# Attention in two halves of the queries: maximum, softmax, values and copies of the result

## The chip, the cores and the metric

The kernel runs on one core of a Trainium2 chip. A core has a matrix engine (TensorE, PE in the profile; its weight loads are listed as PEld), three engines for elementwise work (VectorE or DVE, ScalarE or ACT, GpSimd or POOL) and a queue engine (SyncE or SP) that here only starts transfers; 16 DMA engines move the data. Each engine works through its own instructions in order, and semaphores between them say when an operand is ready or a buffer free. Matrix products are summed in eight PSUM banks of 128 partitions x 512 columns; everything else sits in SBUF or, for larger things, in DRAM. The metric is the time of one execution on the device in microseconds (us), the median of three runs.

## The reference

A decoder trunk of two layers on x (1024 positions x 1024 channels). Layer 0 mixes with a gated short convolution, layer 1 with dilated attention; each is followed by a SwiGLU feed-forward net, with RMS norms in between. The change touches only the attention of layer 1:

```python
qkv = (h @ w_qkv).reshape(bsz, seq, 3, N_HEADS, HEAD_DIM)      # 16 heads of 64
for window, dilation in ((128, 1), (512, 4), (2048, 16)):
    o, l = dilated_branch(q, k, v, rel_bias, window, dilation)  # banded, causal, with a bias by distance
    outs.append(o); lses.append(l)                              # o normalised, l = log of the sum of exponentials
alpha = softmax(lses)                                           # over the three branches
o = sum(alpha * outs)
x = x + o @ w_out
```
Since the branches are weighted by their own sums of exponentials, the result for a query is one softmax over the keys of all three branches together: the sum of exp(score - maximum) * v over the sum of exp(score - maximum).

## The kernel before

Everything outside the attention is the same before and after. A matrix product in fp32 is done as three products of rounded parts: `split` (L135) makes of a tile its high part (a copy on ScalarE, L145) and the low part that is left (a subtract on VectorE, L146), and TensorE adds hi*hi, hi*lo and lo*hi (L373, L374, L375). Weights reach the products through `take` (L174) and `ensure` (L166): a slab is loaded (`load_raw`, SP, L159), split, and taken one slab ahead of its use. SBUF tiles are "pages" from a pool of 41, PSUM tiles "banks" from a ring of 8: whoever wants a bank waits until the one eight before it has been read. The order of the code is the order on each engine.

The attention (L1480) runs heads in 17 slots, n = 0 to 16 (`slot`, L1717). In slot n stand the scores of head n, the softmax and value products of head n-1, and "dense" filler for TensorE, taken in steps from a generator (`other`, `fill`): the value projections, the last projections of q and k, and at the end the first half of the output product (`out_product`), which adds to x with L492.

For one head, with keys on the 128 partitions and the 1024 queries in the columns:

- `scores` (L1561): products of key classes and queries (L1574, L1575) fill banks, and VectorE moves them out with the bias added into four tiles: lf (1024 columns) and lh (512) for the two coarser branches, ld and lp for the finest. While that goes on VectorE takes the maximum of the tiles per column into m (L1599, L1620 to L1625). Then POOL reduces m over the partitions into mb (`partition_all_reduce`, L1628), all 1024 columns at once.
- `softmax` (L1631): five pairs of a subtract of mb on VectorE (L1636) and an exponential on ScalarE (L1637), for lf, lh, ld and two pieces of lp. One pair is issued per step of the next slot up to slot 13 (`LAG`), all five together after that.
- `values` (L1640): products of the exponentials with vx (L1647) into two banks acc[0] and acc[1], one for each half of the queries. Both banks are taken at the start. The order is lf for both halves, lh, then ld and lp. vx holds, for each of 16 key blocks, the values of head a=0, 64 columns of ones, and the values of head a=1, so that a window of 128 columns gives the weighted values of one head in 64 rows and the sum in the other 64. At the end ScalarE takes for both halves the logarithm of the sums into z (L1670) and copies the values into o (L1671), and so frees the banks.
- `finish` (L1674) and `attended` (L1707): z becomes 1/sum by an exponential, o is multiplied with it (L1711), and the pair of heads goes to DRAM (odram, POOL's queue, L1712).

vx is one buffer, filled by `load_values` (L1530) for each pair of heads, on SP: six transfers in pieces of 256 bytes (64 values), the first three into the columns of head a=0, the last three into those of head a=1. The columns of a=0 are free once the first head of the old pair has done its products, those of a=1 only when the second has. On the same queue stand the loads of q and k (`load_kq`, L1539), of the bias (`load_bias`, L1465), of weights, and of finished pairs for the output product (`load_attended`, L1796, the tiles oin). The first four pairs are read at the start of slot 11 and split, one per step, by `halves` (L1839).

Of the kernel before, what the change touches and what calls it, by code (L numbers as in the profile page):

```python
# [52 lines left out]
FILL = (("v", 0), ("v", 1), ("v", 2), ("v", 3), ("qk", 7))  # L53
DENSE = (13,) * 13 + (16, 13, 12, 11)
# [47 lines left out]
def trunk(ctx: ExitStack, tc: tile.TileContext, x, gains_in, cwi, ck, cwo, wqkv, wo, relb,  # L102
# [32 lines left out]
    def split(src, dst=None, eng=nc.vector):  # L135

        w = src.shape[1]
        if dst is None:
            if w <= HALF:
                t = page("w", F32R)  # L140
                dst = t[:, :w], t[:, HALF:HALF + w]
            else:
                dst = page("w_hi", F32R)[:, :w], page("w_lo", F32R)[:, :w]
        hi, lo = dst
        nc.scalar.activation(hi, src, AF.Copy)  # L145
        eng.tensor_tensor(out=lo, in0=src, in1=hi, op=ALU.subtract)  # L146
        return hi, lo

# [25 lines left out]
    def take(key, ahead=1):  # L174
        i = op_state[1]
        assert ops[i][0] == key, (ops[i][0], key)
        ensure(i + ahead)
        op_state[1] += 1
        return made.pop(i)
# [1300 lines left out]
    def attention(norm, qk):  # L1480
# [5 lines left out]
        vx = scope["pool"].tile([128, 16, 192], F32, name="vx", tag="vx", bufs=1)  # L1486
        nc.vector.memset(vx[:, :, 64:128], 1.0)
# [41 lines left out]
        def load_values(p):  # L1529
            src = vdram[p // 2]  # L1530
            for a in range(2):
                off = src.offset + p % 2 * 128 + a * 64
                dims = slice(128 * a, 128 * a + 64)
                nc.sync.dma_start(vx[:, 0:8, dims], bass.AP(src.tensor, off, [[256, 128], [128 * 256, 8], [1, 64]]))
# [26 lines left out]
        def scores(p, a, st):  # L1561
# [40 lines left out]
            for j in range(0, 8, 2):  # L1602
# [22 lines left out]
            nc.vector.tensor_tensor(out=m[:, HALF:], in0=m[:, HALF:], in1=lp[:, HALF:], op=ALU.max)  # L1625
            mb = page("mb")
            st["mb"] = mb
            nc.gpsimd.partition_all_reduce(mb, m, 128, bass_isa.ReduceOp.max)  # L1628
            yield

        def softmax(st):  # L1631
            lf, lh, ld, lp, mb = (st[n] for n in ("lf", "lh", "ld", "lp", "mb"))
            for dst, m in ((lf, mb), (lh, mb[:, HALF:]), (ld, mb),
                           (view(lp, 8, [[32, 16], [1, 24]]), view(mb, 8, [[32, 16], [1, 24]])),
                           (lp[:, HALF:], mb[:, HALF:])):
                nc.vector.tensor_tensor(out=dst, in0=dst, in1=m, op=ALU.subtract)  # L1636
                nc.scalar.activation(dst, dst, AF.Exp)  # L1637
                yield

        def values(p, a, st):  # L1640
            lf, lh, ld, lp = (st[n] for n in ("lf", "lh", "ld", "lp"))
            acc = [bank(), bank()]
# [3 lines left out]
            def mm(ih, off, dims, u, rhs, first=False, last=False):  # L1646
                nc.tensor.matmul(view(acc[ih], off, dims), vx[:, u, 64 * a:64 * a + 128], rhs,  # L1647
                                 start=first, stop=last)

            for ih in range(2):  # L1650
                for r4 in range(4):
# [3 lines left out]
            for r4 in range(4):  # L1655
                mm(1, r4 * 32, kd, 12 + r4, view(lh, r4 * 32, kd))
                if r4 % 2:
                    yield
            for j in range(8):
                off = (j % 4) * 8  # L1660
                mm(j // 4, off, b1, j, view(ld, blk(j), b1), last=False)
                if j:
                    mm(j // 4, off, b1, j - 1, view(lp, blk(j), b1), last=j % 4 == 3)
                yield
            o, z = st["o"], st["z"]
            n0 = slice(64 * a, 64 * a + 64)
            z0 = slice(64 - 64 * a, 128 - 64 * a)
            for ih in range(2):
                s = slice(ih * HALF, (ih + 1) * HALF)
                nc.scalar.activation(z[n0, s], acc[ih][z0], AF.Ln)  # L1670
                nc.scalar.activation(o[n0, s], acc[ih][n0], AF.Copy)  # L1671
            yield
# [44 lines left out]
        def slot(n, dense, ndense, late=0, hook=iter(())):  # L1717

            def other(k):
                for _ in range(k):  # L1720
                    next(dense, None)
# [80 lines left out]
        def split_attended(raw):  # L1802
            return {p: split(t) for p, t in raw.items()}
# [35 lines left out]
        def halves():  # L1839
            for q, t in done.items():  # L1840
                first[q] = split(t)
# [12 lines left out]
        run(dense)  # L1854
        return acts
# [180 lines left out]
```

## Time and profile before

| | us |
|---|---|
| median of three runs | 2103.54 (2102.79, 2103.54, 2103.99) |
| the profiled execution | 2105.08 |
| its span, first to last instruction | 2103.3 |
| TensorE busy | 2083.1 (99%), granted clock 0.998 |
| VectorE, ScalarE, POOL busy | 1746.1 (83%), 1013.7 (48%), 240.0 (11%) |
| the attention's slots | about 1105 to 1475 of the span |

The profile comes from one execution, 1.54 us above the median. A row of a timeline gives start, duration, engine, line of the kernel, operation, output <- inputs with their sizes, how many instructions are drawn together (x8), and in brackets how long the engine stood idle before and on whom it waited. A line of the waits names the waiting instruction, whom it waited for, and the total, the number and the longest of these waits. A row of a group (by line and tile) gives shortest, median and longest duration in ns.

### The profile page before, as it was taken

The numbers are of one execution on the slowest core, as the hardware profiler recorded it, in microseconds if no ns is written. First come the engines' busy times: TensorE is split into PE (matmuls) and PEld (weight loads), VectorE is DVE, ScalarE is ACT, GpSimd is POOL, SyncE is SP. The second block draws the span as 40 slices with busy tenths as digits, with TensorE's granted clock in tenths as the row PEclk, the third lists the DMA queues.
The fourth block names the chain that finished last, engine by engine and source line by source line (L and its number), as shares of the span: only waits on it lengthen the run. The fifth ranks groups of instructions, "written<-read, shape, count | busy, mean of one in ns | idle before, by whom it ended". The sixth has DMA issues, their size and how long they took to land. (4 is left out here: it accounts for less than half of the span.)

```text
span 2103.3 us, 30766 instructions
## 1 busy us (share of the span) xinstructions
PE 2083.1 (99%) x10990; PEld 1792.2 (85%) x10990; DVE 1746.1 (83%) x3264; ACT 1013.7 (48%) x1852; POOL 240.0 (11%) x336
## 2 busy tenths in 40 slices
PE   9999999999999999999999999999999999999998
PEld 7788888888888888887789999988788888888887
DVE  8898769988888788968984778987998888888886
ACT  7433427444444454445553566555544434456433
POOL 1000000110101010010223232211011001001000
PEclk9999999999999999999999999999999999999999
DMA  7322643233333467452658788955223323368432
GB/s 216 100 96 71 230 135 76 101 105 111 102 105 110 145 201 208 133 159 65 232 201 209 161 202 210 250 165 154 71 87 108 107 99 113 110 194 245 158 96 80
DMA packets 141495, 300.70 MB, mean 143 GB/s; under 512 B 48236, under 2 KB 54462, under 8 KB 141344
## 3 DMA queue, kind: packets, MB, share of 16 engines
q1 hardware_dynamic: 107488, 201.94, 32.4%
q0 software_dynamic: 26224, 82.11, 12.6%
q10 hardware_dynamic: 7632, 14.70, 1.9%
q8 instruction: 87, 1.43, 0.3%
q14 instruction: 64, 0.52, 0.1%
HBM read 208.42 MB, written 82.93 MB: 139 GB/s over the span
## 5 line engine op out<-in xcount | busy, mean ns | idle before, releaser
L573 PE MATMUL bank<-b,w 128*128 128x512 f32 x1980 | 772.5, 390 | 5.4 <-DVE w L146 5.2
L571 PE MATMUL bank<-b,w 128*128 128x512 f32 x1980 | 772.3, 390 | 2.3 <-ACT w L145 1.1
L572 PE MATMUL bank<-b,w 128*128 128x512 f32 x1980 | 771.9, 390 | 0.6 <-DVE b L882 0.6
L573 PEld LDWEIGHTS bank<-b,w 128*128 128x128 f32 x1980 | 372.0, 188 | 87.5 <-DVE w L146 10.5
L571 PEld LDWEIGHTS bank<-b,w 128*128 128x128 f32 x1980 | 372.3, 188 | 80.3 <-ACT w L145 1.9
L572 PEld LDWEIGHTS bank<-b,w 128*128 128x128 f32 x1980 | 372.3, 188 | 76.6 <-DVE b L882 1.2
L145 ACT ACTIVATE w<-combo 128x512 fp32r<-128x512 f32 (+2 forms) x492 | 251.5, 541 | 238.9 <-DVE combo L193 219.7
L146 DVE TENSOR_TENSOR w<-combo,w 128x512 fp32r<-128x512 f32 (+2 forms) x492 | 279.8, 582 | 37.8 <-ACT w L145 37.0
L577 ACT ACTIVATE part<-bank 128x512 f32<-128x512 f32 x189 | 112.5, 595 | 383.9 <-PE bank L573 378.7
L146 DVE TENSOR_TENSOR w<-raw,w 128x512 fp32r<-128x512 f32 (+2 forms) x345 | 194.4, 585 | 36.5 <-ACT w L145 36.5
L581 DVE TENSOR_TENSOR part<-part,bank 128x256 f32<-128x256 f32 (+1 forms) x369 | 173.1, 499 | 31.9 <-PE bank L573 17.3
L145 ACT ACTIVATE w<-raw 128x512 fp32r<-128x512 f32 (+2 forms) x345 | 168.5, 531 | 47.8 <-PE bank L573 12.2
L373 PE MATMUL bank<-w_hi,w 128*128 128x512 f32 (+1 forms) x400 | 151.0, 378 | 0.1
L375 PE MATMUL bank<-w_hi,w 128*128 128x512 f32 (+1 forms) x400 | 149.3, 373 | 0.7 <-DVE w L146 0.7
L374 PE MATMUL bank<-w_lo,w 128*128 128x512 f32 (+1 forms) x400 | 149.0, 373 | 0.0
L801 DVE TENSOR_TENSOR x<-x,bank 128x512 f32<-128x512 f32 x136 | 92.9, 683 | 28.7 <-PE bank L573 28.7
L492 DVE TENSOR_TENSOR x<-x,bank 128x512 f32<-128x512 f32 (+1 forms) x104 | 66.7, 644 | 59.8 <-PE bank L375 58.9
L193 DVE TENSOR_TENSOR combo<-raw 128x512 f32<-128x512 f32 (+1 forms) x174 | 112.6, 648 | 0.0
L375 PEld LDWEIGHTS bank<-w_hi,w 128*128 128x128 f32 x400 | 75.3, 188 | 14.8 <-DVE w L146 1.6
L564 DVE TENSOR_TENSOR b<-hin,b 128x512 fp32r<-128x512 f32 x126 | 79.5, 686 | 9.4 <-ACT b L563 9.4
L373 PEld LDWEIGHTS bank<-w_hi,w 128*128 128x128 f32 x400 | 75.5, 189 | 12.3 <-ACT w L145 0.5
L374 PEld LDWEIGHTS bank<-w_lo,w 128*128 128x128 f32 x400 | 75.5, 189 | 11.9
(234 smaller groups left out, 3377.0 us busy)
## 6 DMA issues: line engine op xcount, KB each, us to landing
hin<-part SPq DMA_DIRECT2D x126, 256.0 KB
raw<-in_ffn_w_gate SPq DMA_DIRECT2D x44, 512.0 KB
raw<-in_ffn_w_up SPq DMA_DIRECT2D x44, 512.0 KB
part<-sum POOLq DMA_DIRECT2D x72, 256.0 KB, 2.3
raw<-in_ffn_w_down SPq DMA_DIRECT2D x48, 384.0 KB
raw<-in_attn_w_qkv SPq DMA_DIRECT2D x27, 512.0 KB
raw<-in_conv_w_in SPq DMA_DIRECT2D x24, 512.0 KB
part<-part POOLq DMA_DIRECT2D x36, 256.0 KB, 2.6
```

The costliest lines, as they stand in the source:

```text
L145: nc.scalar.activation(hi, src, AF.Copy)
L146: eng.tensor_tensor(out=lo, in0=src, in1=hi, op=ALU.subtract)
L193: eng.tensor_tensor(out=c, in0=a, in1=b, op=op)
L373: nc.tensor.matmul(b, whi[:, a], ahi[:, s], start=first, stop=False)
L374: nc.tensor.matmul(b, whi[:, a], alo[:, s], start=False, stop=False)
L375: nc.tensor.matmul(b, wlo[:, a], ahi[:, s], start=False, stop=last)
L571: nc.tensor.matmul(b, hi[:, a], bhi, start=start and k == 0, stop=False, skip_group_check=True)
L572: nc.tensor.matmul(b, hi[:, a], blo, start=False, stop=False, skip_group_check=True)
L573: nc.tensor.matmul(b, lo[:, a], bhi, start=False, stop=k == n - 1, skip_group_check=True)
L577: nc.scalar.activation(t, b, AF.Copy)
L581: nc.vector.tensor_tensor(out=t, in0=t, in1=b, op=ALU.add)
L801: nc.vector.tensor_tensor(out=X[n][:, half(h)], in0=X[n][:, half(h)], in1=b, op=ALU.add)
```

## The change

Four things change, all within the attention.

*Halves of the queries.* The maximum is reduced in two pieces of 512 columns: the first as soon as ld and lp of queries 0 to 511 are in m, in the middle of the scores, the second after the last scores. The softmax becomes seven pairs instead of five, in the order lf, ld, lp of half 0, then lf, lh, ld, lp of half 1. The value products go by halves too: acc[0] is taken, gets lf, ld and lp, and its z and o follow at once; only then acc[1] is taken.

*Values in 512-byte pieces.* vx is laid out as ones, head 0, head 1, ones, head 0, and so on, with 17 blocks of ones, so that the 128 values of a pair lie side by side. `load_values` is three transfers instead of six, in pieces of 512 bytes. Sums and values change rows, and z and o with them.

*Low parts later.* While the attention runs, the subtract of a `split` is put on a list and issued at the next filler step or the next `take`.

*Reads of finished pairs.* oin of pairs 0 and 1 is read and split in slot 10, that of 2 and 3 in slot 11, in SP's order behind the loads of q, k and bias of that slot.

```diff
@@ split @@
         nc.scalar.activation(hi, src, AF.Copy)
-        eng.tensor_tensor(out=lo, in0=src, in1=hi, op=ALU.subtract)
+        low = lambda: eng.tensor_tensor(out=lo, in0=src, in1=hi, op=ALU.subtract)
+        if behind[0]:
+            lows.append(low)
+        else:
+            low()
...
+    behind, lows = [False], []
+
+    def flush_lows():
+        while lows:
+            lows.pop(0)()
@@ take @@
+        flush_lows()
         ensure(i + ahead)
+        if i + 1 > state0:
+            flush_lows()
@@ attention, load_values @@
-        vx = scope["pool"].tile([128, 16, 192], F32, name="vx", tag="vx", bufs=1)
-        nc.vector.memset(vx[:, :, 64:128], 1.0)
+        vx = scope["pool"].tile([128, 16 * 192 + 64], F32, name="vx", tag="vx", bufs=1)
+        nc.vector.memset(view(vx, 0, [[192, 17], [1, 64]]), 1.0)
...
-            for a in range(2):
-                off = src.offset + p % 2 * 128 + a * 64
-                dims = slice(128 * a, 128 * a + 64)
-                nc.sync.dma_start(vx[:, 0:8, dims], bass.AP(src.tensor, off, [[256, 128], [128 * 256, 8], [1, 64]]))
-                for h in range(2):
-                    nc.sync.dma_start(vx[:, 8 + 4 * h:12 + 4 * h, dims],
-                                        bass.AP(src.tensor, off + 512 * 256 * h, [[1024, 128], [256, 4], [1, 64]]))
+            off = src.offset + p % 2 * 128
+            nc.sync.dma_start(view(vx, 64, [[192, 8], [1, 128]]),
+                              bass.AP(src.tensor, off, [[256, 128], [128 * 256, 8], [1, 128]]))
+            for h in range(2):
+                nc.sync.dma_start(view(vx, (8 + 4 * h) * 192 + 64, [[192, 4], [1, 128]]),
+                                  bass.AP(src.tensor, off + 512 * 256 * h, [[1024, 128], [256, 4], [1, 128]]))
@@ scores @@
                     nc.vector.tensor_tensor(out=q(m), in0=q(m), in1=q(lp), op=ALU.max)
+                    mb = page("mb")
+                    st["mb"] = mb
+                    nc.gpsimd.partition_all_reduce(mb[:, :HALF], m[:, :HALF], 128, bass_isa.ReduceOp.max)
...
-            mb = page("mb")
-            st["mb"] = mb
-            nc.gpsimd.partition_all_reduce(mb, m, 128, bass_isa.ReduceOp.max)
+            nc.gpsimd.partition_all_reduce(mb[:, HALF:], m[:, HALF:], 128, bass_isa.ReduceOp.max)
@@ softmax @@
-            for dst, m in ((lf, mb), (lh, mb[:, HALF:]), (ld, mb),
+            for dst, m in ((lf[:, a], mb[:, a]), (ld[:, a], mb[:, a]),
                            (view(lp, 8, [[32, 16], [1, 24]]), view(mb, 8, [[32, 16], [1, 24]])),
-                           (lp[:, HALF:], mb[:, HALF:])):
+                           (lf[:, b], mb[:, b]), (lh, mb[:, b]), (ld[:, b], mb[:, b]), (lp[:, b], mb[:, b])):
@@ values @@
-            acc = [bank(), bank()]
+            acc = {}
...
             for ih in range(2):
+                acc[ih] = bank()
                 for r4 in range(4):
                     mm(ih, r4 * 32, kd, 8 + r4, view(lf, ih * HALF + r4 * 32, kd), first=r4 == 0)
...
+                for r4 in range(4 * ih):
+                    mm(1, r4 * 32, kd, 12 + r4, view(lh, r4 * 32, kd))
...
+                for j in range(4 * ih, 4 * ih + 4):
+                    off = (j % 4) * 8
+                    mm(ih, off, b1, j, view(ld, blk(j), b1), last=False)
+                    if j:
+                        mm(ih, off, b1, j - 1, view(lp, blk(j), b1), last=j % 4 == 3)
                     yield
...
+                nc.scalar.activation(z[n0, half(ih)], acc[ih][n0], AF.Ln)
+                nc.scalar.activation(o[n0, half(ih)], acc[ih][o0], AF.Copy)
                 yield
@@ slot @@
             def other(k):
                 for _ in range(k):
+                    flush_lows()
                     next(dense, None)
...
                 bias[n + 1] = load_bias(n + 1)
+            done.update(load_attended(ps))
@@ the loop over the slots @@
+        behind[0] = True
         for n in range(H):
-            if n == LAG - 2:
-                done.update(load_attended(range(AO)))
-            hook = halves() if n == LAG - 2 else iter(())
-            slot(n, dense, DENSE[n], 3 if n == H - 2 else 0, hook)
+            ps = {OIN - 1: (0, 1), OIN: (2, 3)}.get(n, ())
+            hook = halves(ps)
+            slot(n, dense, DENSE[n], 3 if n == H - 2 else 0, hook, ps)
```

How the order moves is shown at three places. The first is ScalarE from slot 13 into slot 14, with the exponentials of head 13 and z and o of head 12. Before (lf_12950 to lp_12953 are head 13's; banks 13058 and 13059 are head 12's two halves):

```order
L1637 ACTIVATE lf_12950<-lf_12950 128x1024
L1637 ACTIVATE lh_12951<-lh_12951 128x512
L1637 ACTIVATE ld_12952<-ld_12952 128x1024
L1637 ACTIVATE lp_12953<-lp_12953 128x16x24
L1637 ACTIVATE lp_12953<-lp_12953 128x512
L145 ACTIVATE w_13100<-raw_12869 128x512
L1670 ACTIVATE z_12947<-bank_13058 64x512
L1671 ACTIVATE o_12946<-bank_13058 64x512
L1670 ACTIVATE z_12947<-bank_13059 64x512
L1671 ACTIVATE o_12946<-bank_13059 64x512
```
After (lf_12990 to lp_12993 are head 13's; banks 13103 and 13129 are head 12's halves):

```order
L1684 ACTIVATE z_12987<-bank_13103 64x512
L1685 ACTIVATE o_12986<-bank_13103 64x512
L1652 ACTIVATE lf_12990<-lf_12990 128x512
L1652 ACTIVATE ld_12992<-ld_12992 128x512
L1652 ACTIVATE lp_12993<-lp_12993 128x16x24
L1652 ACTIVATE lf_12990<-lf_12990 128x512
L1652 ACTIVATE lh_12991<-lh_12991 128x512
L1652 ACTIVATE ld_12992<-ld_12992 128x512
L1652 ACTIVATE lp_12993<-lp_12993 128x512
L146 ACTIVATE w_13149<-raw_12912 128x512
L1684 ACTIVATE z_12987<-bank_13129 64x512
L1685 ACTIVATE o_12986<-bank_13129 64x512
```
z and o of the first half have moved ahead of all exponentials of head 13; those of the second half still stand behind them and behind a weight's copy.

The second place is VectorE over the end of the same head's scores (m is the maximum per column, mb the reduced one, bias rows are evictions of banks). Before:

```order
L1611 TENSOR_TENSOR ld_12952<-bank_13029,bias_12752 128x16x16
L1616 TENSOR_TENSOR lp_12953<-bank_13029,bias_12752 128x16x16
L1611 TENSOR_TENSOR ld_12952<-bank_13039,bias_12752 128x16x16
L1616 TENSOR_TENSOR lp_12953<-bank_13039,bias_12752 128x16x8
L1624 TENSOR_TENSOR m_12988<-m_12988,ld_12952 128x512
L1625 TENSOR_TENSOR m_12988<-m_12988,lp_12953 128x512
L492 TENSOR_TENSOR x_12778<-x_12778,bank_13010 128x512
L1636 TENSOR_TENSOR lf_12950<-lf_12950,mb_13051 128x1024
```
After (the first half's all-reduce waits for the first row shown; lines are 13 higher, softmax's 15):

```order
L1635 TENSOR_TENSOR m_13028<-m_13028,lp_12993 128x16x24
L147 TENSOR_TENSOR w_13045<-raw_12522,w_13045 128x512
L1651 TENSOR_TENSOR ld_12797<-ld_12797,mb_12879 128x512
L1624 TENSOR_TENSOR ld_12992<-bank_13073,bias_12790 128x16x16
L1629 TENSOR_TENSOR lp_12993<-bank_13073,bias_12790 128x16x16
L1651 TENSOR_TENSOR lp_12798<-lp_12798,mb_12879 128x512
L1624 TENSOR_TENSOR ld_12992<-bank_13085,bias_12790 128x16x16
L1629 TENSOR_TENSOR lp_12993<-bank_13085,bias_12790 128x16x8
L1640 TENSOR_TENSOR m_13028<-m_13028,ld_12992 128x512
L1641 TENSOR_TENSOR m_13028<-m_13028,lp_12993 128x512
L506 TENSOR_TENSOR x_12816<-x_12816,bank_13049 128x512
L1651 TENSOR_TENSOR lf_12990<-lf_12990,mb_13064 128x512
```
Head 12's last subtracts (ld_12797, lp_12798) and a weight's low part now stand between the start of the first reduce and the last four evictions of head 13's scores.

The third place is SP's queue in slot 11. Before:

```order
L1799 DMA oin<-odram_85 128x1024
L1799 DMA oin<-odram_86 128x1024
L1799 DMA oin<-odram_87 128x1024
L1799 DMA oin<-odram_88 128x1024
L1546 DMA ka<-kq_1_2926 64x1024
L1547 DMA ka<-kq_1_2926 64x1024
L1534 DMA vx<-vdram_95 128x8x64
L1536 DMA vx<-vdram_95 128x4x64 x2
L1534 DMA vx<-vdram_95 128x8x64
L1536 DMA vx<-vdram_95 128x4x64 x2
```
After (the first row is the last load of slot 10):

```order
L1815 DMA oin<-odram_86 128x1024
L170 DMA raw<-in_attn_w_out 128x512 x2
L1559 DMA ka<-kq_1_2926 64x1024
L1560 DMA ka<-kq_1_2926 64x1024
L1546 DMA vx<-vdram_95 128x8x128
L1549 DMA vx<-vdram_95 128x4x128 x2
L1564 DMA qa<-kq_0_2925 64x1024 x2
L1565 DMA ql_10192<-kq_0_2925 64x1024
L1482 DMA bias<-tables 128x1x361
L1483 DMA bias<-tables 128x1x349
L1815 DMA oin<-odram_87 128x1024
L1815 DMA oin<-odram_88 128x1024
```
Three rows of vx stand where six did (a row x2 counts for two), and two of the four loads of finished pairs come at the end of the slot instead of ahead of it.

More of the change, by code (lines that the diff above doesn't have):

```diff
@@ L53 @@
 FILL = (("v", 0), ("v", 1), ("v", 2), ("v", 3), ("qk", 7))
+OIN = LAG - 2
 DENSE = (13,) * 13 + (16, 13, 12, 11)
@@ L1715, in attention, with slot @@
         OZ, acts = {}, {}
-        def slot(n, dense, ndense, late=0, hook=iter(())):
+        def slot(n, dense, ndense, late=0, hook=iter(()), ps=()):
             def other(k):
                 for _ in range(k):
+                    flush_lows()
                     next(dense, None)
@@ L1802, in split_attended @@
         def split_attended(raw):
-            return {p: split(t) for p, t in raw.items()}
+            done = {p: split(t) for p, t in raw.items()}
+            flush_lows()
+            return done
         def out_product(g, ps, acts):
@@ L1837, in fill, with halves @@
             yield from out_product(0, range(AO), first)
-        def halves():
-            for q, t in done.items():
-                first[q] = split(t)
+        def halves(ps):
+            for q in ps:
+                first[q] = split(done.pop(q))
                 yield
         dense = fill()
+        behind[0] = True
         for n in range(H):
-            if n == LAG - 2:
-                done.update(load_attended(range(AO)))
-            hook = halves() if n == LAG - 2 else iter(())
-            slot(n, dense, DENSE[n], 3 if n == H - 2 else 0, hook)
+            ps = {OIN - 1: (0, 1), OIN: (2, 3)}.get(n, ())
+            hook = halves(ps)
+            slot(n, dense, DENSE[n], 3 if n == H - 2 else 0, hook, ps)
             run(hook)
@@ L1854, in attention @@
         run(dense)
+        flush_lows()
+        behind[0] = False
         return acts
```

26 lines of the change are left out of this document (8 added, 18 removed).

## The prediction

> **What bounds the kernel now.** I read the page's busy times first, then the waits of TensorE inside the attention, then busy time by stretch, then the timelines around the one place where TensorE stands still, and last VectorE's waits and the DMA shares, since the change touches these.
>
> ```profile
> span 2103.3 us, 30766 instructions
> PE 2083.1 (99%) x10990; PEld 1792.2 (85%) x10990; DVE 1746.1 (83%) x3264; ACT 1013.7 (48%) x1852; POOL 240.0 (11%) x336
> ```
> TensorE is busy for 99% of the span. The change neither adds nor drops a matmul, so it can only win idle time of TensorE, and only inside the attention (about 1105 to 1475 us). How much is there?
>
> ```profile
> PE bank L1574 <- ACT o L1671: 0.8, 1, 0.8
> ...
> 1145.00:1300.00 155.00, 155.00 (x1291) 152.70 (x1290) 118.74 (x222) 93.15 (x132) 47.95 (x39) 1.00 0.76 183
> 1300.00:1350.00 50.00, 50.00 (x344) 45.92 (x343) 47.41 (x76) 30.42 (x41) 14.55 (x10) 1.00 1.02 262
> ...
> 1365.00:1370.00 5.00, 4.24 (x35) 3.97 (x34) 4.09 (x7) 4.80 (x9) 0.00 (x0) 1.00 0.55 126
> ...
> 1403.00:1405.00 2.00, 1.96 (x14) 1.47 (x13) 2.00 (x4) 1.84 (x3) 0.00 (x0) 1.00 0.24 82
> ...
> sum 370.00, PE 369.21 PEld 346.26 DVE 285.09 ACT 208.19 POOL 90.40; mean PE 46.15 PEld 43.28 DVE 35.64 ACT 26.02 POOL 11.30
> ```
> The first line is the only wait that TensorE has there. The others are busy times by stretch (PE, weight loads, DVE, ACT, POOL, clock, DMA share, GB/s): 370.00 - 369.21 = 0.79 us idle in the whole attention, 0.76 of it between 1365 and 1370. The granted clock is 1.00 throughout, so nothing is to be won there. VectorE is full only in 1300:1350, 47.41 of 50.00 us, where the DMA is saturated too (share 1.02).
>
> The idle 0.76 us, on TensorE, ScalarE, VectorE and POOL in turn:
>
> ```profile
> 1367.28 1.05 PE L1647 MATMUL bank<-lf,vx 128*128 128x128 f32 x8
> 1369.09 0.33 PE L1574 MATMUL bank<-qa,kca 128*128 128x128 f32 x1 [0.76 <-ACT o L1671]
> ...
> 1363.70 1.06 ACT L1637 ACTIVATE lf<-lf 128x1024 f32<-128x1024 f32 x1 [5.39 <-DVE lf L1636]
> 1366.40 1.03 ACT L1637 ACTIVATE lp<-lp 128x384 f32<-128x384 f32 x2
> 1367.34 0.61 ACT L145 ACTIVATE w<-raw 128x512 fp32r<-128x512 f32 x1
> 1367.86 0.58 ACT L1670 ACTIVATE z<-bank 64x512 f32<-64x512 f32 x1
> 1368.44 0.59 ACT L1671 ACTIVATE o<-bank 64x512 f32<-64x512 f32 x1
> ...
> 1358.33 0.69 DVE L1625 TENSOR_TENSOR m<-m,lp 128x512 f32<-128x512 f32 x1
> 1362.44 1.23 DVE L1636 TENSOR_TENSOR lf<-lf,mb 128x1024 f32<-128x1024 f32 x1 [2.82 <-POOL mb L1628]
> ...
> 1359.18 3.22 POOL L1628 PARTITION_ALL_REDUCE mb<-m  x1 [13.12 <-DVE m L1625]
> ```
> The last row of head 13's maximum ends at 1359.02. POOL's all-reduce takes 3.22 us, VectorE waits 2.82 for it, ScalarE 5.39, and head 13's five exponentials stand ahead of head 12's z and o in ScalarE's order. So the bank of head 12's first query half comes free at 1368.44 + 0.59 = 1369.03, and the scores of head 14 start at 1369.09.
>
> **The change, part by part.** *Order on ScalarE.* Now z and o of head 12's first half stand ahead of head 13's exponentials, and that bank is wanted one bank later in the ring. Those of the second half stay behind seven exponentials and a weight copy, but this bank is only wanted by head 13's second half, taken after scores that now start at 1369.09. When are they done? The second half's all-reduce starts near 1359.2 and takes between 1.6 us (half of 3.22, if it goes by columns) and 3.22 (if it is all fixed cost), then four subtracts, one exponential, the weight copy and z and o:
>
> ```profile
> L1636 DVE TENSOR_TENSOR lf<-lf,mb x16: 1209/1226/1227, 1136.4 to 1401.6; 128x1024 f32<-128x1024 f32 x16
> L1636 DVE TENSOR_TENSOR lh<-lh,mb x16: 681/682/687, 1138.2 to 1402.7; 128x512 f32<-128x512 f32 x16
> ...
> L1637 ACT ACTIVATE lf<-lf x16: 1050/1061/1065, 1137.7 to 1402.8; 128x1024 f32<-128x1024 f32 x16
> L1637 ACT ACTIVATE lh<-lh x16: 612/632/635, 1139.0 to 1403.8; 128x512 f32<-128x512 f32 x16
> ```
> 4 x 0.68 + 0.63 + 0.61 + 0.58 + 0.59 = 5.1, so 1365.9 to 1367.5: 1.6 us or more before 1369.09. The stall goes: **-0.76 us**. The idle 0.04 us at 1403 (TensorE meets the last head's exponentials) should go too, since the last head's first half is ready sooner: -0.04, which I round to a sum of -0.8.
>
> *More instructions.* Per head lf and ld become two pieces each: VectorE pays 2 x (2 x 0.682 - 1.22) = +0.29 us, ScalarE 2 x (2 x 0.632 - 1.061) = +0.41, over 16 heads 4.6 and 6.5 us. Cover: of the 370 us VectorE works 285.09 and ScalarE 208.19. That cover is thin only in 1300:1350, with 2.59 us of VectorE left for three heads, of which 0.9 is now taken. What VectorE gains there against it:
>
> ```profile
> DVE lf L1636 <- POOL mb L1628: 32.9, 13, 3.5
> ...
> L1628 POOL PARTITION_ALL_REDUCE mb<-m x16 | 55.9, 3496 | 142.8 <-DVE m L1625 81.7 <-PE bank L1647 22.9 <-PE bank L1519 14.0
> ```
> It waits 32.9 us for the maximum in 13 heads; with the first half reduced during the scores most of that goes, which is worth nothing to TensorE but pays for the extra pieces. POOL's 16 reduces become 32: between +0 and +55.9 us; POOL is busy for 90.40 of 370 us, so 0 either way.
>
> *All-reduce beside VectorE.* This speaks against the change: VectorE slows down while POOL reduces.
>
> ```profile
> 1343.19 2.08 DVE L146 TENSOR_TENSOR w<-raw,w 128x512 fp32r<-128x512 f32 x1
> 1345.20 0.67 DVE L492 TENSOR_TENSOR x<-x,bank 128x512 f32<-128x512 f32 x1
> ...
> 1342.84 3.22 POOL L1628 PARTITION_ALL_REDUCE mb<-m  x1 [9.76 <-DMA vx<-vdram]
> ...
> 1320.71 6.32 DVE L146 TENSOR_TENSOR w_lo<-oin,w_hi 128x1024 fp32r<-128x1024 f32 x4
> 1320.97 4.05 POOL L1628 PARTITION_ALL_REDUCE mb<-m  x1 [1.85 <-DVE m L1625]
> ```
> A 512-column subtract takes 2.08 us beside the reduce against the 0.68 of lh: +1.4. Four of 1024 columns take 6.32 against 4 x 1.22: +1.4 too. The x addition with one PSUM operand, also beside it, takes its usual 0.67. So two-operand SBUF work is held for about 1.4 us. Before, VectorE mostly had nothing to do then but wait for the maximum; now the first half's reduce falls among head n's last scores, where max, low parts and head n-1's subtracts stand ahead of the evictions that free banks. The price for TensorE lies between 0 and 16 x 1.4 = 22 us. I take **0**: the hold at 1343 lay in the fullest stretch of VectorE and cost TensorE nothing (50.00 of 50.00 busy), and that is the nearest row. The Trainium skill says of this, in "GPSIMD Engine Reference", Specifications, that POOL's SBUF interface is shared with VectorE, with contention for instructions that have two SBUF inputs. The trace agrees (2.08 against 0.67); by the page each further reduce costs VectorE time, which is the rival below.
>
> *Moved loads of odram (oin).* Pairs 0 and 1 load one slot sooner. Two of the four splits (6.32 / 2 = 3.2 us of VectorE) leave 1300:1350 for the slot ahead, where VectorE is at 118.74 of 155 us. That more than pays for the 0.9 above. On SP two loads fewer stand ahead of slot 11's ka and vx, which is worth up to 1 us to transfers and nothing to TensorE.
>
> *Low parts later.* A subtract issues one filler step later. Cover: `take` makes the weights one slab ahead, and an out-product slab is 24 matmuls long (two halves, four pairs, three products), some 24 x 0.23 = 5.5 us by the starts of neighbouring products (1401.71, 1401.94, 1402.16). If the cover were gone TensorE would wait one subtract, 0.68 us, for a slab: 0 to 5 us for the 8 slabs; I take 0.
>
> ```profile
> 1401.71 0.39 PE L373 MATMUL bank<-w_hi,w 128*128 128x512 f32 x1
> 1401.94 0.39 PE L374 MATMUL bank<-w_lo,w 128*128 128x512 f32 x1
> 1402.16 0.39 PE L375 MATMUL bank<-w_hi,w 128*128 128x512 f32 x1
> ```
> *Values in 512-byte pieces.* One transfer now carries both heads, so nothing of it starts before the last value product of the pair before; head 0's half used to start earlier.
>
> ```profile
> 1301.99 0.58 SPq L1534 DMA_DIRECT2D vx<-vdram  x1
> 1307.82 1.63 SPq L1534 DMA_DIRECT2D vx<-vdram  x1
> 1344.04 0.38 SPq L1534 DMA_DIRECT2D vx<-vdram  x1
> ...
> 1318.31 0.94 PE L1647 MATMUL bank<-lf,vx 128*128 128x128 f32 x7
> 1353.84 1.05 PE L1647 MATMUL bank<-lf,vx 128*128 128x128 f32 x8
> ...
> DMA packets 2237, 0.81 MB, mean 163 GB/s; under 512 B 2108, under 2 KB 2108, under 8 KB 2237
> q1 hardware_dynamic: 2237, 0.81, 67.0%
> ```
> The first row is head 0's half, the second and third the release of all in two pairs; their first products follow 10.5 and 9.8 us later. The last two rows are 1377 to 1382 us, nearly all 256-byte packets: 0.67 x 5 us x 16 / 2237 = 24 ns each. A half is 512 KB, 2048 such packets, 3.1 us. Afterwards 2048 pieces of 512 bytes follow the release. If a piece costs the same, they take the 3.1 us of the late half before: no delay. If it costs by bytes, 48 ns, they take 6.2 us, 3.1 more; since head 1's half was in time before, they come between 6.7 us early and 3.1 us late. Only in the two reloads in saturated 1300:1350 can that bite: 0 to 6.2 us. I take 0, since even 6.2 leaves 3.6 us of 9.8 for what else is queued, and the packets of the early half are gone from that queue. On SP, qa and ql stand behind the same release before and after. The Trainium skill gives a fixed overhead of 3 cycles per packet over 32-byte beats ("DMA: Bandwidth & Descriptors", Why small descriptors are slow): 11 cycles for 256 bytes and 19 for 512. By that a piece is an estimated 42 ns, the reload 5.3 us and still in time; no run here shows it.
>
> **The sum.** -0.8 + 0 = -0.8 us. The profiled execution took 2105.08 (span 2103.3 and 1.78 around it), 1.54 above the median of 2103.54; so 2104.3 for it, and **2102.7** for the median. What a measurement can tell from no change is about 0.2%, 4.2 us: 2099.3 to 2107.7.
>
> **Rivals.**
> - *VectorE held by the first half's reduce (slower).* For: the 2.08 us row, and 47.41 of 50 us busy in 1300:1350. Against: VectorE loses a wait of up to 3.5 us per head and two splits there. It decides once the hold, 1.4 us, outlasts TensorE's lead over the evictions. With the three heads of 1300:1350 fully paid: 3 x 1.4 - 0.8 = +3.4, 2106.9; with five heads +6.2, 2109.7.
> - *Values late (slower).* For: the saturated share of 1.02. Against: the slack of 9.8 us. It decides where a piece costs by bytes and the queue adds over 3.6 us. Two reloads, each late by up to 3.1: 2105.8 for half of it, 2108.9 for all.
> - *No change of the end.* The bank wait only moves, to the second half's z and o: if each half's reduce is as dear as the whole and VectorE is held as well, 1367.5 + 1.4 = 1368.9, just before the need. Then 2103.5. For: ScalarE still has seven exponentials ahead of them. Against: the need is after 1369.09.
>
> **How the numbers follow.** Stall gone, all else covered: 0.50, own range 2101.7 to 2103.7 (the spread of the runs). No change of the end: 0.13. VectorE held: 0.22, of which 0.12 above 2107.7. Values late: 0.12, of which 0.06 above. Something that TensorE's idle 0.79 us does not show, faster by over 0.2%: 0.03. So faster 0.03, slower 0.18, the same 0.79. The range runs from 2101.5 (the stall, 0.3 us of slack at its edges and the runs' spread) to 2108.9 (the late values in full); it leaves out about 0.16, mostly VectorE held in five heads or more.
>
> **What would show it.** Right: no wait of TensorE for z or o between 1365 and 1370; VectorE's 32.9 us for the maximum mostly gone; two reduces per head of 1.6 to 3.2 us each; value products with no wait for vx. Wrong: a wait of TensorE for an eviction (lf, lh, ld, lp) while the first half's reduce runs, a first value product that waits for vx, or a product that waits for a low part.

## The result and the profile after

The changed kernel takes 2106.37 us (20 runs, 2105.70 to 2112.23) against 2103.45 (20 runs, 2102.22 to 2104.99): a ratio of 1.0016 with a 95% interval of 1.0010 to 1.0022 (ratios and intervals come from all executions, so they are not quite the quotient of the two medians, here 1.0014). That is 2.9 us slower, where 0.8 us faster was forecast. Five of the changed kernel's twenty executions lie between 2107.6 and 2112.3, and all twenty count.

The page's busy times, and TensorE's waits in 1105 to 1420 us, of the changed kernel:

```profile
PE 2082.6 (99%) x10990; PEld 1792.5 (85%) x10990; DVE 1751.5 (83%) x3296; ACT 1019.0 (48%) x1884; POOL 250.0 (12%) x352
...
PE bank L1662 <- ACT lp L1652: 2.3, 2, 1.5
PE bank L1662 <- ACT ld L1652: 0.7, 1, 0.7
```
The old wait for head 12's bank (0.8 us) is gone. In its place TensorE waits three times, 3.0 us in all, at value products (L1662) for exponentials (L1652). The busy time by stretch, with the same columns and stretches as before, says where:

```profile
1145.00:1300.00 155.00, 151.94 (x1265) 149.45 (x1264) 118.95 (x229) 93.68 (x147) 52.31 (x47) 1.00 0.70 185
1300.00:1350.00 50.00, 50.00 (x344) 45.81 (x342) 47.36 (x86) 33.05 (x48) 16.42 (x13) 1.00 0.80 225
...
1365.00:1370.00 5.00, 5.00 (x38) 4.66 (x37) 4.38 (x7) 4.06 (x7) 0.00 (x0) 1.00 0.66 166
...
sum 370.00, PE 366.94 PEld 344.11 DVE 288.78 ACT 212.23 POOL 100.19; mean PE 45.87 PEld 43.01 DVE 36.10 ACT 26.53 POOL 12.52
```
TensorE idles for 3.06 us in 1145:1300, which was full before and where VectorE is busy for only 118.95 of 155 us. The full stretch 1300:1350 stays full, and 1365:1370 is full now. The attention's idle time has gone from 0.79 to 370.00 - 366.94 = 3.06 us, +2.3 of the +2.9; the other 0.6 is no larger than what single executions differ by, and I do not assign it. (The spans of the two profiled executions, 2104.8 and 2103.3 us, differ by only 1.5, because the one before lay 1.54 above its median.)

How do the exponentials come late, with VectorE a quarter idle? The timelines of TensorE, ScalarE and VectorE at the two places, after:

```profile
1163.58 0.28 PE L1532 MATMUL bank<-w_lo,b 128*128 128x256 f32 x1
...
1166.51 0.49 PE L1662 MATMUL bank<-ld,vx 128*128 128x128 f32 x2 [0.74 <-ACT ld L1652]
1167.77 0.49 PE L1662 MATMUL bank<-lp,vx 128*128 128x128 f32 x2 [0.78 <-ACT lp L1652]
1217.26 1.06 PE L1662 MATMUL bank<-lf,vx 128*128 128x128 f32 x8
...
1220.97 0.49 PE L1662 MATMUL bank<-lp,vx 128*128 128x128 f32 x2 [1.53 <-ACT lp L1652]
...
1165.83 0.63 ACT L1652 ACTIVATE ld<-ld 128x512 f32<-128x512 f32 x1 [4.99 <-DVE ld L1651]
1167.09 0.63 ACT L1652 ACTIVATE lp<-lp 128x512 f32<-128x512 f32 x1 [0.64 <-DVE lp L1651]
1220.29 0.63 ACT L1652 ACTIVATE lp<-lp 128x512 f32<-128x512 f32 x1 [4.21 <-DVE lp L1651]
...
1163.96 1.23 DVE L147 TENSOR_TENSOR w_lo<-raw,w_hi 128x1024 fp32r<-128x1024 f32 x1 [2.99 <-PE bank L1532]
1165.11 0.69 DVE L1651 TENSOR_TENSOR ld<-ld,mb 128x512 f32<-128x512 f32 x1
1166.38 0.68 DVE L1651 TENSOR_TENSOR lp<-lp,mb 128x512 f32<-128x512 f32 x1
1218.42 1.23 DVE L147 TENSOR_TENSOR w_lo<-raw,w_hi 128x1024 fp32r<-128x1024 f32 x1 [2.35 <-PE bank L1662]
1219.57 0.68 DVE L1651 TENSOR_TENSOR lp<-lp,mb 128x512 f32<-128x512 f32 x1
```
Read from the bottom up: VectorE stands for 2.99 and 2.35 us before the low part of a 1024-column weight slab (L147), and it waits for TensorE. Both operands are there (w_hi ended at 1160.32 and at 1214.57, by the timeline of ScalarE). What is missing must then be the page that w_lo is to be written to. The profile names L1532 as the releaser at 1163.96, and the last product that reads the w_lo of an earlier slab ran from 1163.58 to 1163.86; at 1218.42 it names L1662, and the products that read the second half of lf, of the head in progress, ran from 1217.26 to 1218.32. That it is the page is inferred here; the run with one page more, below, tests it. In VectorE's order the last one or two softmax subtracts stand behind this low part, so ScalarE's exponentials are late, and TensorE, whose products had kept the page busy, waits for them in turn. Before, the same slab's low part waited 1.23 us for its own high part on ScalarE and not for TensorE, and the last subtract behind it was in time (before, near the first place):

```profile
1163.13 1.23 DVE L146 TENSOR_TENSOR w_lo<-raw,w_hi 128x1024 fp32r<-128x1024 f32 x1 [1.23 <-ACT w_hi L145]
1164.27 0.68 DVE L1636 TENSOR_TENSOR lp<-lp,mb 128x512 f32<-128x512 f32 x1
```

The two reduces, by line, and the softmax's subtracts of the changed kernel (shortest, median and longest duration in ns):

```profile
L1638 POOL PARTITION_ALL_REDUCE mb<-m x16: 1777/2033/2088, 1129.5 to 1396.4; - x16
...
L1642 POOL PARTITION_ALL_REDUCE mb<-m x16: 1783/2152/2687, 1131.9 to 1399.5; - x16
...
L1651 DVE TENSOR_TENSOR lf<-lf,mb x32: 672/684/1529, 1131.8 to 1403.9; 128x512 f32<-128x512 f32 x32
```
Half the columns take 2.03 to 2.15 us, about two thirds of the 3.22 of the whole, and VectorE's 32.9 us of waiting for the maximum are gone from its waits.

### The profile page after: what moved, and what is told of

It is laid out like the page before. It is cut to its first block, busy times and chain, and to the rows that moved or that the text cites. A ratio compares the mean times of both kernels' runs of the same rounds, so it can differ in the third digit from the quotient of the medians.

```text
span 2104.8 us, 30820 instructions
## 1 busy us (share of the span) xinstructions
PE 2082.6 (99%) x10990; PEld 1792.5 (85%) x10990; DVE 1751.5 (83%) x3296; ACT 1019.0 (48%) x1884; POOL 250.0 (12%) x352
## 4 chain that ended last, share of the span: by engine, by line
PE 49%; DVE 3%; ACT 1%; issue 0%; DVEq 0%; ACTq 0%
PE bank L587 9%; PE bank L586 9%; PE bank L585 9%; PE bank L1662 4%; PE bank L387 2%; PE bank L388 2%; PE bank L389 2%; PE bank L1531 1%; PE bank L1532 1%; PE bank L1533 1%; PE bank L1588 1%; PE bank L1587 1%; PE bank L677 1%; PE bank L680 1%; PE bank L679 1%; DVE w L147 1%
## 5 line engine op out<-in xcount | busy, mean ns | idle before, releaser
L147 DVE TENSOR_TENSOR w<-combo,w 128x512 fp32r<-128x512 f32 (+2 forms) x492 | 279.7, 582 | 37.8 <-ACT w L146 37.0
L147 DVE TENSOR_TENSOR w<-raw,w 128x512 fp32r<-128x512 f32 (+2 forms) x345 | 192.2, 578 | 36.2 <-ACT w L146 36.2
```

Source lines behind the costliest of these rows:

```text
L147: low = lambda: eng.tensor_tensor(out=lo, in0=src, in1=hi, op=ALU.subtract)
```

## The experiments

Each is the changed kernel with one edit, unless it says otherwise, timed over 5 to 11 executions beside the kernel before on the same chip. The diffs are cut (...) and stand against the changed kernel. Three theories were put against each other first: the *page theory* (the early mb takes a page, w_lo gets one that TensorE still reads, the softmax is queued behind it), the *deferral theory* (the low part is late because it is put on a list), and the *too-many-pairs theory* (seven pairs end too late in the slot).

**One maximum again.** The halves of softmax and values stay.

```diff
-                    mb = page("mb")
-                    st["mb"] = mb
-                    nc.gpsimd.partition_all_reduce(mb[:, :HALF], m[:, :HALF], 128, bass_isa.ReduceOp.max)
...
-            nc.gpsimd.partition_all_reduce(mb[:, HALF:], m[:, HALF:], 128, bass_isa.ReduceOp.max)
+            mb = page("mb")
+            st["mb"] = mb
+            nc.gpsimd.partition_all_reduce(mb, m, 128, bass_isa.ReduceOp.max)
```


> The changed kernel with the maximum reduced in one piece of 1024 columns at the end of the scores, as before, and its page mb taken only then; all else as changed. Page theory (the early mb takes the free page, so that a weight's low part gets a page which TensorE is still reading; VectorE waits there, with head n-1's last softmax subtracts queued behind): VectorE's waits of 2.99 us (near 1161) and 2.35 us (near 1216) for TensorE go, TensorE's 3.0 us of waits for the exponentials of ld and lp fall under 0.5, time 2102.4 to 2103.8 against 2106.4. Deferral theory (the low part is late because it is put on a list): waits and time stay, 2106. Too-many-pairs theory (seven pairs in eight steps end too late for the second half's products): waits stay or grow, since the maximum now comes later, 2106 to 2109.

Measured: 2103.09 us against 2103.31 (ratio 1.0000, 0.9991 to 1.0008). The low parts at both places, the wait for the maximum and TensorE's waits:

```profile
1160.09 1.22 DVE L147 TENSOR_TENSOR w_lo<-raw,w_hi 128x1024 fp32r<-128x1024 f32 x1
...
1213.22 1.22 DVE L147 TENSOR_TENSOR w_lo<-raw,w_hi 128x1024 fp32r<-128x1024 f32 x1
...
DVE lf L1650 <- POOL mb L1641: 35.9, 13, 3.6
...
PE bank L1587 <- ACT o L1684: 0.4, 1, 0.4
PE bank L1661 <- ACT lp L1651: 0.3, 1, 0.3
```
Neither low part waits, and the loss is gone although the maximum comes later and VectorE waits 35.9 us for it. That excludes both rivals as the whole cause: the list and the seven pairs are still there. The changed kernel's loss needs the early maximum.

**Low parts at once.**

```diff
         dense = fill()
-        behind[0] = True
```


> The changed kernel with each low part issued at once again; all else as changed. Deferral theory: VectorE's two waits for TensorE and TensorE's 3.0 us of waits for ld and lp go, 2102.4 to 2103.5. Page theory: the low part still gets a page just read by the value products in at least one of the two slots, so a wait of 1 to 2 us remains, 2104.5 to 2106.5. Too-many-pairs theory: nothing changes, 2106.4.

Measured: 2111.09 us (ratio 1.0038, 1.0025 to 1.0050), worse than the changed kernel by 4.7 us where the deferral theory had it better by 3. Also more than the page theory expected. VectorE's low parts at three places, and TensorE's waits:

```profile
1160.98 1.23 DVE L147 TENSOR_TENSOR w_lo<-raw,w_hi 128x1024 fp32r<-128x1024 f32 x1 [1.48 <-ACT w_hi L146]
...
1207.72 1.23 DVE L147 TENSOR_TENSOR w_lo<-raw,w_hi 128x1024 fp32r<-128x1024 f32 x1 [1.95 <-ACT w_hi L146]
...
1218.07 1.23 DVE L147 TENSOR_TENSOR w_lo<-raw,w_hi 128x1024 fp32r<-128x1024 f32 x1 [2.35 <-PE bank L1662]
...
PE bank L1662 <- ACT lp L1652: 3.3, 3, 1.5
PE bank L1662 <- ACT ld L1652: 2.3, 2, 1.8
```
At once, a low part also waits for its own high part on ScalarE (1.48 and 1.95 us), with the softmax behind it; and the wait for the page is as it was at 1218. (The kernel before has such waits too, 1.23 us at 1163 and 1.76 at 1207, and TensorE lost nothing by them.) So the list does not cause the loss; with the halves in place it saves 4.7 us. The deferral theory falls. Of the 4.7 us, 5.6 - 3.0 = 2.6 are longer waits of TensorE; some 1.6 more are its clock, by the run of the halves alone, below.

**One slab less loaded ahead.**

```diff
-        load_raw(i + ahead)
+        load_raw(i + (1 if behind[0] else ahead))
```


> The changed kernel with weights loaded one slab ahead instead of two while the attention runs, which leaves one more page free there; order of work on the engines as changed. Page theory: VectorE's waits of 2.99 and 2.35 us and TensorE's waits for ld and lp go (under 0.5 us left), 2102.4 to 2103.8, unless the later weight loads cost a wait of their own, which would stand in TensorE's waits for w. Deferral theory and too-many-pairs theory: all stays, 2106.4 or more.

Measured: 2109.36 us (ratio 1.0030, 1.0018 to 1.0041). The wait for the page is gone, but a weight now lands late (ScalarE, VectorE, TensorE):

```profile
1217.54 1.06 ACT L146 ACTIVATE w_hi<-raw 128x1024 fp32r<-128x1024 f32 x1 [6.53 <-DMA raw<-in_attn_w_qkv]
...
1218.63 1.23 DVE L147 TENSOR_TENSOR w_lo<-raw,w_hi 128x1024 fp32r<-128x1024 f32 x1 [5.16 <-ACT w_hi L146]
...
PE bank L1662 <- ACT ld L1652: 3.5, 1, 3.5
```
As a test of the page it is spoiled, since it put another wait at the same instruction. It shows the rest of the chain, though: whatever that low part waits for (here a load, 5.16 us), the softmax behind it is late and TensorE pays (3.5 us).

**Low parts later still.**

```diff
-            lows.append(low)
+            lows.append([low, 4 if w > HALF else 1])
...
-    def flush_lows():
-        while lows:
-            lows.pop(0)()
+    def flush_lows(step=9):
+        while lows:
+            lows[0][1] -= step
+            if lows[0][1] > 0:
+                break
+            lows.pop(0)[0]()
...
-                    flush_lows()
+                    flush_lows(1)
                     next(dense, None)
```


> The changed kernel with the low parts of the 1024-column weight slabs put off by four filler steps instead of one, so that they stand behind the last softmax subtract of the slot. The page is as late as before, but what is queued behind it is not the softmax. Page theory and deferral theory, as far as the queue on VectorE is the link: TensorE's waits for ld and lp under 0.5 us, 2102.4 to 2103.8; VectorE may still wait for TensorE 1 to 3 us. Too-many-pairs theory: waits for lp stay, 2106.4.

Measured: 2105.83 us (ratio 1.0012, 1.0003 to 1.0020). VectorE's order at the first place, and TensorE's only wait in the attention:

```profile
1160.79 0.69 DVE L1654 TENSOR_TENSOR ld<-ld,mb 128x512 f32<-128x512 f32 x1
1162.05 0.87 DVE L1654 TENSOR_TENSOR lp<-lp,mb 128x512 f32<-128x512 f32 x1
1164.69 1.22 DVE L147 TENSOR_TENSOR w_lo<-raw,w_hi 128x1024 fp32r<-128x1024 f32 x1
...
PE bank L391 <- DVE w_lo L147: 2.1, 1, 2.1
```
With the subtracts ahead of the low part no product waits for ld or lp, as it should be if the queue on VectorE is the link. The time is not won: the edit also put off the low parts of oin, which are 1024 columns wide too, and one of these now comes 2.1 us late to its own product (L391, at 1331).

**One page more.** m gets a buffer of its own, paid for by two half pages; the instructions of every engine and their order are those of the changed kernel.

```diff
-            m = page("m")
+            m = scope["pool"].tile([128, 1024], F32, name="m", tag="m", bufs=1)
...
-        scope["halves"] = 8
+        scope["halves"] = 6
         acts = attention(norm, qk)
```


> The changed kernel with the tile m (maximum per column) in a buffer of its own instead of a page, paid for by two of the eight half pages; each engine's instructions and their order are as changed, and one page more is free in each slot. Page theory: VectorE's waits of 2.99 and 2.35 us for TensorE go, TensorE's 3.0 us for ld and lp fall under 0.5, time 2102.2 to 2103.5. If the first half's reduce does the harm in another way (its hold on VectorE, or seven pairs in eight steps), the waits stay, 2105.5 to 2106.5. If six half pages are too few, a wait for one shows and the time is over 2104 without any wait for ld or lp.

Measured: 2103.92 us (ratio 1.0001, 0.9992 to 1.0009).

```profile
1160.04 1.22 DVE L147 TENSOR_TENSOR w_lo<-raw,w_hi 128x1024 fp32r<-128x1024 f32 x1
...
1213.17 1.40 DVE L147 TENSOR_TENSOR w_lo<-raw,w_hi 128x1024 fp32r<-128x1024 f32 x1
...
PE bank L1662 <- ACT lp L1652: 0.9, 1, 0.9
PE bank L1587 <- ACT kca L1571: 0.6, 1, 0.6
```
The first two lines are VectorE at the two places: both waits are gone, with the same early reduce, the same list and the same seven pairs. This is what the page theory rests on. The time is 0.4 us over the expected range: TensorE waits for lp and for kca, at 1341 and 1324, in the stretch that was full before.

**The halves alone**: the other three parts of the change are undone.

```diff
-        vx = scope["pool"].tile([128, 16 * 192 + 64], F32, name="vx", tag="vx", bufs=1)
+        vx = scope["pool"].tile([128, 16, 192], F32, name="vx", tag="vx", bufs=1)
...
-            ps = {OIN - 1: (0, 1), OIN: (2, 3)}.get(n, ())
-            hook = halves(ps)
+            if n == LAG - 2:
+                done.update(load_attended(range(AO)))
+            hook = halves() if n == LAG - 2 else iter(())
...
-        behind[0] = True
```


> The kernel before with the halves of the queries alone (maximum, softmax, values, z and o): values in 256-byte pieces, low parts at once, oin in slot 11 as before. Page theory, with low parts at once as in the run without the list: waits for ld and lp as there, 2109 to 2112. If the 512-byte pieces or the oin order took part in the loss, less than that: 2103 to 2108.

Measured: 2115.43 us (ratio 1.0054, 1.0040 to 1.0068), with seven waits for ld and lp, and a stretch in which TensorE's granted clock falls (0.77, behind the busy times):

```profile
PE bank L1663 <- ACT lp L1653: 4.2, 4, 1.5
PE bank L1663 <- ACT ld L1653: 2.8, 3, 1.7
...
1220.00:1235.00 15.00, 12.90 (x84) 12.72 (x85) 11.93 (x23) 8.78 (x14) 5.17 (x6) 0.77 0.59 163
```
The loss is the halves' own, and it is 12 us without the rest of the change, 3 us more than any theory had. The theories counted waits alone, and these are 7.0 us. The clock adds to them: it is 1.00 in this stretch before and after the change and 0.77 here, some 15 x 0.23 = 3.4 us of a full clock (an estimate from this row), directly behind two waits of 1.75 and 0.78 us. The low parts at once and the slab less show 0.89 there, some 1.6 us, behind 1.76 and 0.78 and behind 3.53 and 0.57 us, and the low parts later still 0.57 in 1331:1335, some 1.7 us, behind the 2.1. Single waits of up to 1.53 us, the changed kernel's among them, left it at 1.00. That the waits lower the clock is read from this order; no run tests it by itself.

Nor is the page the only wait here: one low part waits for it (2.33 us at 1218), others wait for their own high part (1.34 us at 1161, 1.96 at 1208). With the longer softmax queued behind it, any late low part reaches TensorE. The other parts together save 9 of the 12 us, the list 4.7 of them by the run above. Which of the 512-byte pieces and the moved loads saves the rest was not tried.

**All but the halves** (one maximum, five pairs, old order of the products):

```diff
-            for dst, m in ((lf[:, a], mb[:, a]), (ld[:, a], mb[:, a]),
+            for dst, m in ((lf, mb), (lh, mb[:, HALF:]), (ld, mb),
...
-                acc[ih] = bank()
+            acc.update({0: bank(), 1: bank()})
```


> The changed kernel with the halves of the queries undone (one maximum, five pairs, values in the old order); 512-byte pieces, low parts a step later and the oin loads as changed. Page theory: no wait for ld or lp; the old 0.8 us at head 12's bank stays, so 2103.0 to 2104.0, as before. If late values or the moved loads cost something: over 2104.5, with a wait for vx or w in TensorE's waits.

Measured: 2103.79 us against 2103.65 (ratio 1.0003, 0.9994 to 1.0012).

```profile
PE bank L1587 <- ACT o L1685: 0.7, 1, 0.7
PE bank L1661 <- DVE lp L1629: 0.6, 1, 0.6
```
The old wait for the bank is there (0.7), nothing waits for vx or for a weight. The other three parts by themselves cost nothing and bring nothing that this measurement can tell.

**The maximum in halves from head 10 on**, where no 1024-column weight slab is split any more:

```diff
-                    mb = page("mb")
-                    st["mb"] = mb
-                    nc.gpsimd.partition_all_reduce(mb[:, :HALF], m[:, :HALF], 128, bass_isa.ReduceOp.max)
+                    if 2 * p + a >= 10:
+                        mb = page("mb")
+                        st["mb"] = mb
+                        nc.gpsimd.partition_all_reduce(mb[:, :HALF], m[:, :HALF], 128, bass_isa.ReduceOp.max)
```
(and below it the second half for these heads, the whole for the others.)

> The changed kernel with the maximum in two pieces only for heads 10 to 15, in one for heads 0 to 9, where the 1024-column weight slabs are split. Page theory: neither the waits for ld and lp near 1166 and 1221 nor the old 0.8 us near 1369, so the lowest time of all, 2102.0 to 2102.8. If the hold of VectorE by the first half's reduce costs TensorE something in the full stretch 1300 to 1350: an eviction's wait there, over 2103.5.

Measured: 2102.64 us against 2103.65 (ratio 0.9995, 0.9986 to 1.0004), with no wait of TensorE in the attention at all (the sum over the same eight stretches):

```profile
sum 370.00, PE 370.00 PEld 346.90 DVE 289.90 ACT 215.84 POOL 92.85; mean PE 46.25 PEld 43.36 DVE 36.24 ACT 26.98 POOL 11.61
```
It ran once more:

> The kernel with the maximum in two pieces only for heads 10 to 15, once more, to see whether it stands below the kernel before: 2102.2 to 2103.0 against 2103.3 to 2103.7, and no wait of TensorE in the attention. If the first result was chance: within 0.3 us of the kernel before.

Measured: 2102.78 us against 2103.40 (ratio 0.9995, 0.9986 to 1.0004). Its profiled execution had one wait:

```profile
PE bank L1668 <- ACT lp L1658: 0.8, 1, 0.8
```
So even this order has little to spare near 1340, where VectorE is nearly full, and the wait comes in one execution and not in another.

**The maximum in halves alone**, with five pairs, the old order of the products, and the other three parts of the change (the edit of the softmax and values in the run on all but the halves, without that of the maximum).

> The changed kernel with five softmax pairs and the old order of the value products (both banks at the start, lf of both halves, lh, then ld and lp), but with the maximum still reduced in two pieces; 512-byte pieces, low parts and oin as changed. If the early page alone decides: VectorE waits 2 to 3 us for TensorE at a weight's low part, and TensorE 1 to 3 us for lp, 2104.5 to 2106.5. If it takes both, the late page and the second half's ld and lp coming two pairs later in the slot: VectorE may wait, TensorE waits under 0.5 us for ld and lp, 2102.8 to 2104.0.

Measured: 2102.45 us against 2103.40 (ratio 0.9998, 0.9990 to 1.0007). TensorE waits for nothing in 1105 to 1480. VectorE's order at the two places:

```profile
1158.44 0.68 DVE L1651 TENSOR_TENSOR lp<-lp,mb 128x512 f32<-128x512 f32 x1
1160.90 1.22 DVE L147 TENSOR_TENSOR w_lo<-raw,w_hi 128x1024 fp32r<-128x1024 f32 x1
...
1210.74 0.68 DVE L1651 TENSOR_TENSOR lp<-lp,mb 128x512 f32<-128x512 f32 x1
1213.87 1.70 DVE L147 TENSOR_TENSOR w_lo<-raw,w_hi 128x1024 fp32r<-128x1024 f32 x1
```
Two things differ from the changed kernel: the low part does not wait, and with five pairs the last subtract stands ahead of it (1158.44 before 1160.90), so that a wait would have hurt nothing. The branch that was expected, VectorE waiting without harm, did not show. So the early reduce makes the loss only together with the longer softmax or the later end of lf (or both); these two were not separated.

## Why the prediction was wrong

- *The stall at 1369 goes: right, with its timing off.* After, TensorE does not wait there and 1365:1370 is full. On ScalarE:

```profile
1362.30 0.57 ACT L1684 ACTIVATE z<-bank 64x512 f32<-64x512 f32 x1
1363.39 0.62 ACT L1652 ACTIVATE lf<-lf 128x512 f32<-128x512 f32 x1
...
1368.50 0.59 ACT L1685 ACTIVATE o<-bank 64x512 f32<-64x512 f32 x1
```
The first half's z and o run ahead of all exponentials of head 13. The second half's are done at 1368.50 + 0.59 = 1369.09, not between 1365.9 and 1367.5, because the second reduce started at 1361.62 and not near 1359.2. That cost nothing, since their bank was not wanted yet. The estimate of -0.8 us fits the two orders without the new waits, 2102.64 and 2102.78, and 2102.45, against 2103.40 to 2103.65, but each interval reaches 1, so a gain is not shown.
- *More instructions, covered by idle time: the step that failed.* The size was about right: over the whole execution VectorE's busy time rose from 1746.1 to 1751.5 us and ScalarE's from 1013.7 to 1019.0, 5.4 and 5.3 where 4.6 and 6.5 were worked out. The cover was wrong. "That cover is thin only in 1300:1350" was read from busy time, so the longer softmax was put at 0. The loss fell into 1145:1300, where VectorE is busy for 77%: 3.0 us of TensorE's waits. The sum asked how much work VectorE has, and not what stands ahead of the last subtracts in its order. That is the low part of a weight, and it waits.
- *The page of mb* stood in no term of the sum. Taking mb earlier in the scores was costed as a reduce on POOL and as a hold on VectorE, not as one of 41 pages held longer. With the early page the low part waits 2.99 and 2.35 us; with one page more, in the same order, it does not.
- *Low parts later, taken as 0: right in effect.* No product waited for a low part, and without the list the changed kernel is 4.7 us slower; without the halves, the list and the other two parts change nothing. But the term asked only who waits for a low part (one subtract, 0.68 us). What the low part itself waits for, and who is queued behind it, was the question that mattered.
- *All-reduce beside VectorE, taken as 0: right in effect.* A 512-column subtract beside a reduce took up to 1.53 us against 0.68, so the hold is there (0.85), and no product of the changed kernel waited for an eviction. The Trainium skill's row on the shared SBUF interface ("GPSIMD Engine Reference", Specifications) fits this again. As a rival it gave 2106.9, close to the measured 2106.37 by luck: no eviction was late, and the loss came by another road.
- *Values late: did not happen.* No run shows a wait of TensorE for vx. (The rival's "late by up to 3.1" is late against before; against the need the prediction's own figures leave 3.6 us.)
- *A reduce of half the columns* took 2.03 to 2.15 us, within the bounds of 1.6 and 3.2.
- *No change of the end*: did not happen; the bank's wait did not move. Its time for the second half's z and o, 1368.9, was nearly met (1369.09), but no product stood waiting for that bank.

## What to carry to other kernels

An instruction that is moved or made to follow another must be asked three things: what it waits for, counting the buffer it writes to, who waits for it, and who stands behind it in its engine's order. Where a pool of buffers is nearly used up, as here, taking a tile some microseconds earlier can give another tile a buffer that the busiest engine still reads, and an engine that is a quarter idle can then hold up work that it has time for. Busy shares by stretch did not show this here; the order on the engine, with the distance from each result to its use, did.

## What the runs showed of the hardware

A reduce over the partitions of 512 columns takes 2.03 to 2.15 us in the median against 3.22 for 1024, so cutting it in two costs about 1 us of POOL's time per head, here hidden. A wait also travels: 2.35 us on VectorE became 1.53 us on TensorE at 1221, because the subtract that was blocked fed an exponential that fed the product. And a wait can cost more than its length: in the four traces where TensorE waited 2.1 to 4.1 us in all within 5 us, its granted clock fell right behind it (to 0.77 over 15 us with the halves alone); behind shorter waits in the attention it did not.
